# Spreading a row over 128 partitions with one-hot matmuls and ScalarE copies in place of GpSimd's partition broadcast

## The chip, the cores and the metric

The kernel runs on one core of a Trainium2 chip. The metric is the device time of one execution in microseconds (us), from the device's own clock. The kernel before takes 2005.57 us (median of 3 runs, 2004.93 to 2007.7).

Engine names in the profile: PE is TensorE (matmul), PEld its weight loads, DVE VectorE, ACT ScalarE, POOL GpSimd, SP SyncE, which here only issues DMAs. L1267 is line 1267 of the kernel.

## The reference

Two blocks run one after the other on 256 tokens of width 1024, all in float32. The first block is two hybrid layers (a gated convolution, latent attention and dilated attention, merged by gates). The second is one transformer block with conditioning, and it is the one that matters here:

```
mod = silu(c) @ w_ada + b_ada                    # one row of 6*1024
sh1, sc1, gt1, sh2, sc2, gt2 = split(mod, 6)     # six rows of 1024
h = rms_norm(x, g_attn) * (1 + sc1) + sh1
x = x + gt1 * (concat(gqa(h), diff_att(h)) @ w_o)
h2 = rms_norm(x, g_ffn) * (1 + sc2) + sh2
x = x + gt2 * moe(h2)                            # 32 experts, top 4 of each token
return rms_norm(x, g_final)
```

The rows gt1, sh2, (1 + sc2)*g_ffn, gt2 and g_final are each one row of 1024 that multiplies or is added to every token. Tokens lie on the 128 partitions (two tiles of 128 tokens), so each of these rows has to stand in all 128 partitions.

## The kernel before

One instruction stream per engine; each engine takes its instructions in order and waits on semaphores. The order within an engine is made by a scheduler at build time, from priorities and an estimate of times, so an edit can move instructions far from it.

**Where the rows come from.** A side task (`ada`) forms the six rows beside the first block. Four of them end in a tile `modr` of 128 x 2 x 512, zero but for the partitions 0, 32, 64 and 96: partition 32*j holds one half row for each of two slots. `mod_row(i, dst)` (L850) spreads a row to all partitions in two halves of 512 with GpSimd's `partition_broadcast` (L854). Five rows are spread, in nine broadcasts:

- gt1 into the buffer `M`, at the start of the second block (`mod_row(0, ...)`, L1049, just behind the first projection);
- sh2 into `sh` and (1+sc2)*g_ffn into `a`, near the end of the grouped-query attention, when two work tiles come free (`mod_row(1, ...)`, `mod_row(2, ...)`);
- gt2 into `kaT` and `va` at the start of the expert part (L1267). GpSimd then multiplies the experts' output bias `bi` by it (L1269);
- g_final into a weight buffer that has just come free (L1306), beside the last pair of experts.

**What GpSimd does besides.** It computes the reciprocal square root of each token's norm as a power of -0.5: `rm` at L129 (for the block's first norm and for the router, one instruction for each token tile) and `rs_p` at L137.

**The second block.** First norm of both tiles (`rm`, then `XM` scaled by it on VectorE at L227), transposes of `XM` on TensorE (L243), projections, the two attentions, the output projection, the router for tile 0 and tile 1 (`router`, L1158 on), and the expert part. In the router VectorE needs `rm` for the modulated row (`vb`, L1203) and for the logits (`lg`, L1189); the choice of experts and the dispatch matmuls (L1356), which gather each expert's tokens into `xT`, follow from these. Where a row is printed, `mk` is the mask of chosen experts, `sl` their slots, `tri` a triangle matrix for a running count.

**The expert part.** Sixteen pairs of experts; each needs 24 weight tiles of 1 MB, which SyncE loads in a fixed order (L1250, `mload`) into 19 buffers (`mv`, `mhch`, `mhcl`, `mXM`, `mr`, `mw` and so on) in turn. Most of these are work tiles of the second block, and a load waits until its buffer has been read for the last time. TensorE takes the tiles in the same order: 16 input tiles for both experts (L1368), SwiGLU on VectorE and ScalarE, 8 output tiles (L1448; in the last pair L1438), and the combination by gates (L1293).

PSUM has four banks under the tag `mm` for all projections, scores and dispatch matmuls; the expert part holds two of them for the pair in work (L1332 puts the input bias in with a one-hot matmul).

Of the kernel before, what the change touches and what calls it, by code (L numbers as in the profile page):

```python
# [8 lines left out]
F32 = mybir.dt.float32  # L9
# [3 lines left out]
AF = mybir.ActivationFunctionType  # L13
# [10 lines left out]
NEW, TB, YB = 3, 2, 1  # L24
# [5 lines left out]
class Net:  # L30
# [739 lines left out]
    def ada(self):  # L770
# [76 lines left out]
        nc.vector.scalar_tensor_tensor(sc2, sc2, 1.0, grow, op0=ALU.add, op1=ALU.mult)  # L847
        yield

    def mod_row(self, i, dst):  # L850
        nc = self.nc
        for j in range(2):
            r, jj = i // 2, (i % 2) * 2 + j
            nc.gpsimd.partition_broadcast(dst[:, j * 512:(j + 1) * 512], self.modr[32 * jj:32 * jj + 1, r, :],  # L854
                                          channels=128)

    def kv_proj(self, hh, hl, src):
        nc, tmp, wq = self.nc, self.tmp, self.d["w_qkv"]
# [399 lines left out]
    def moe(self, ctx):  # L1258
        tc, nc, d = self.tc, self.nc, self.d
        T = self.tmp = ctx.enter_context(tc.tile_pool(name="moet", bufs=2))  # L1260
        P = ctx.enter_context(tc.tile_pool(name="moe", bufs=1))
        new = [P.tile([128, 2048], F32, name=f"mw{i}") for i in range(NEW)]
        rg = [self.ring.tile([128, 2048], F32, name="mr", tag="raw") for _ in range(3)]
        self.mbufs += rg + new + ["Y1"]
        gt2 = [self.kaT, self.va.rearrange("p b n -> p (b n)")]
        for h in range(2):
            nc.gpsimd.partition_broadcast(gt2[h], self.modr[32 * h + 64:32 * h + 65, 1, :], channels=128)  # L1267
            bh = self.bi[0:32, h * 512:(h + 1) * 512]
            nc.gpsimd.tensor_tensor(bh, bh, gt2[h][0:32], op=ALU.mult)  # L1269
        sl, gt = self.sl, self.gt  # L1270
        self.h2 = self.bigs["vb"].rearrange("p (t n) -> p t n", t=2)
        gT = P.tile([32, 2, 128], F32, name="gT")
        yp = ctx.enter_context(tc.tile_pool(name="yps", bufs=1, space=PSUM))
        acc = [[yp.tile([128, 512], F32, name=f"y{t}{h}") for h in range(2)] for t in range(2)]

        def base():
            p = self.mm_ps([32, 2, 128])
            for t in range(2):
                nc.tensor.transpose(p[:, t], gt[:, t], self.ident)
            nc.scalar.activation(gT, p, AF.Copy)  # L1280
            for t in range(2):
                for h in range(2):
                    hs = slice(h * 512, (h + 1) * 512)
                    nc.tensor.matmul(acc[t][h], self.ident, self.x[:, t, hs], start=False, stop=False)
                    nc.tensor.matmul(acc[t][h], gT[:, t], self.bi[0:32, hs], start=False, stop=False)

        hp = self.hp0
        steps = self.dispatch_steps(sl[:, :, 0:2], gt[:, :, 0:2])
        disp = next(steps)
        for q in range(16):  # L1290
            nxt = None if q in (QO, 15) else (sl[:, :, 2 * q + 2:2 * q + 4], gt[:, :, 2 * q + 2:2 * q + 4])
            disp, hp = self.pair(disp, nxt, [self.onehot(min(2 * q + i, 31)) for i in range(3)], hp, self.mtile, gt2,
                                 lambda t, h, a, b: nc.tensor.matmul(acc[t][h], a, b, start=(q == 0), stop=(q == 15)),  # L1293
                                 steps if q == 0 else (), q == 15)
            if q == 0:
                self.counts()
                base()
            if q == QO:
                while self.mn < 24 * q + 24 + len(self.mbufs) - 1:
                    self.mload()  # L1300
                self.overflow(P, gt2, acc)
                hp = self.in_bias(self.onehot(2 * q + 2))
                disp = self.dispatch(*(v[:, :, 2 * q + 2:2 * q + 4] for v in (sl, gt)))
        buf = self.mbufs[self.mn % len(self.mbufs)]
        gfin, junk = buf[:, 0:1024], buf[:, 1024:1536]
        nc.gpsimd.partition_broadcast(gfin, self.bi[96:97], channels=128)  # L1306
        h2 = self.h2
        ss = [T.tile([128, 2], F32, name="ss", tag="rss", bufs=2) for _ in range(2)]
        square = lambda t, h: nc.scalar.activation(junk, acc[t][h], AF.Square, scale=0.03125, accum_out=ss[t][:, h:h + 1])
        hs = [slice(0, 512), slice(512, 1024)]  # L1310
        for t in range(2):
            square(t, 0)
            nc.vector.tensor_tensor(h2[:, t, hs[0]], gfin[:, hs[0]], acc[t][0], op=ALU.mult)
        for t in range(2):
            square(t, 1)
            r = self.rmean(T, ss[t])
            nc.vector.tensor_tensor(h2[:, t, hs[1]], gfin[:, hs[1]], acc[t][1], op=ALU.mult)
            nc.scalar.activation(h2[:, t, hs[0]], h2[:, t, hs[0]], AF.Copy, scale=r)
            nc.vector.tensor_scalar(h2[:, t, hs[1]], h2[:, t, hs[1]], r, None, op0=ALU.mult)  # L1319
            for h in range(2):  # L1320
                nc.sync.dma_start(self.out[0, t * 128:(t + 1) * 128, hs[h]], h2[:, t, hs[h]])
# [74 lines left out]
    def pair(self, disp, nxt, oh, hp, tile_of, gt2, acc, steps=(), last=False):  # L1396
        nc, T = self.nc, self.tmp
        xT, gs = disp
        hs = [slice(0, 64), slice(64, 128)]
        for k in range(8):  # L1400
            if k == 4:
                for _ in steps:
                    pass
            self.in_tile(hp, xT, tile_of(), k, hs[0])
        ln0 = self.swiglu(hp)
        hp = self.in_bias(oh[1])
        aT = []
        for k in range(8):
            mm = self.in_tile(hp, xT, tile_of(), k, hs[1])
            if k == 2:  # L1410
                with self.tc.issue_after(mm.ins):
                    aT.append(self.act_T(ln0, last))
                    gsT = T.tile([128, 2, 128], F32, name="gsT", tag="gsT", bufs=1)
                    p = self.mm_ps([128, 2, 128])
                    for t in range(2):
                        nc.tensor.transpose(p[:, t], gs[:, t].rearrange("p e c -> p (e c)"), self.ident)  # L1416
                    nc.scalar.activation(gsT, p, AF.Copy)
        ln1 = self.swiglu(hp)
        hp = None
        if nxt is not None:  # L1420
            with self.tc.issue_after(mm.ins):
                nxt = self.dispatch(*nxt)
        aT.append(self.act_T(ln1, last))
        yp = [self.mm_ps([128, 512]) for _ in range(2)]
        ys = T.tile([128, 2, 512], F32, name="ys", tag="ys", bufs=YB)

        def combine(h):
            nc.vector.tensor_tensor(ys[:, h], gt2[h], yp[h], op=ALU.mult)  # L1428
            for t in range(2):
                acc(t, h, gsT[:, t], ys[:, h])  # L1430

        for f in range(4):
            w = [tile_of() for _ in range(2)]
            if last:
                h, q = divmod(f, 2)
                for c in range(4):
                    for e in range(2):
                        nc.tensor.matmul(yp[h][hs[e]], aT[e][:, c, hs[q]], w[e][:, c * 512:(c + 1) * 512],  # L1438
                                         start=(q == 0 and c == 0), stop=(q == 1 and c == 3))
                if q == 1:  # L1440
                    combine(h)
                continue
            for cc in range(2):
                c, q = (f * 2 + cc) % 4, f // 2
                for h in range(2):
                    for e in range(2):
                        o = cc * 1024 + h * 512
                        nc.tensor.matmul(yp[h][hs[e]], aT[e][:, c, hs[q]], w[e][:, o:o + 512],  # L1448
                                         start=(f == 0 and cc == 0), stop=(f == 3 and cc == 1))
        if nxt is not None:  # L1450
            hp = self.in_bias(oh[2])
        if not last:
            for h in range(2):
                combine(h)
        return nxt, hp
# [161 lines left out]
```

## Time and profile before

| | us |
|---|---|
| median of 3 runs | 2005.57 |
| profiled execution, its time | 2004.15 |
| profiled execution, span of the trace | 2002.5 |
| TensorE busy | 1907.1 (95%) |
| VectorE busy | 916.5 (46%) |
| ScalarE busy | 609.9 (30%) |
| GpSimd busy | 411.6 (21%) |
| DMA, expert part from slice 25 of 40 on | 420 to 421 GB/s |

The profile's page gives busy times of the whole span. TensorE's share is modelled: matmuls overlap, so it shows when TensorE had something in work and not how fast it was. The timeline gives one engine's or all engines' instructions in order of start; what stands in brackets is how long the engine had been idle before, and what ended it, `issue` where no semaphore in the profile did. The windows give the busy time of each engine in a stretch, the mean granted clock of TensorE as a share of 2.4 GHz, and what the DMA engines moved.

### The profile page before, as it was taken

Reading aid. Unit: us, or ns where it says so; the run is one execution under the profiler, and the core shown is the slowest. Engines: PE = TensorE matmul, PEld = TensorE weight load, DVE = VectorE, ACT = ScalarE, POOL = GpSimd, SP = SyncE. Lnnn points to the kernel's source line nnn. Section 1 sums busy time; section 2 is a strip of 40 time slices with the busy share of each in tenths; the row PEclk is TensorE's granted clock in tenths of the full one; section 3 lists DMA queues with packets and bytes.
Section 4 is the critical chain, followed back from the end, with each engine's and each line's share of the span. In section 5 each row is a group of like instructions: output and inputs, shape, how many; then the busy total and the mean of one; then the engine's idle time right before and its main releaser. Section 6 shows DMA issues by size and latency. Waiting matters only on the chain. (4 is left out here: it accounts for less than half of the span.)

```text
span 2002.5 us, 25915 instructions
## 1 busy us (share of the span) xinstructions
PE 1907.1 (95%) x10323; PEld 1182.0 (59%) x10323; DVE 916.5 (46%) x1728; ACT 609.9 (30%) x1099; POOL 411.6 (21%) x334
## 2 busy tenths in 40 slices
PE   6989999989899999889978999999999998999997
PEld 6878988978679889776654333333333333433332
DVE  6798778588976665768762011111111101111102
ACT  4646445546465454545551000000000000100001
POOL 3135336663345235411220000000000000000000
PEclk8999999999999999989998999999999999999999
DMA  6544544645556444544567999999999999999997
GB/s 225 185 140 159 190 158 148 211 168 198 171 169 212 137 160 159 192 148 147 168 231 291 407 380 421 421 420 420 421 421 421 420 421 420 420 421 421 421 421 291
DMA packets 138452, 568.59 MB, mean 284 GB/s; under 512 B 10603, under 2 KB 16747, under 8 KB 90198
## 3 DMA queue, kind: packets, MB, share of 16 engines
q1 hardware_dynamic: 129664, 540.69, 69.9%
q0 software_dynamic: 6912, 25.17, 3.8%
q8 instruction: 83, 1.36, 0.3%
q10 hardware_dynamic: 1750, 1.03, 0.2%
q14 instruction: 43, 0.35, 0.0%
HBM read 565.79 MB, written 1.05 MB: 283 GB/s over the span
## 5 line engine op out<-in xcount | busy, mean ns | idle before, releaser
L158 DVE TENSOR_TENSOR wl<-raw,wh 128x1024 fp32r<-128x1024 f32 (+3 forms) x255 | 339.2, 1334 | 126.8 <-ACT wh L156 123.0
L156 ACT ACTIVATE wh<-raw 128x1024 fp32r<-128x1024 f32 (+3 forms) x255 | 262.8, 1034 | 236.5 <-PE mm L181 217.1
L182 PE MATMUL mm<-hh,wl 128*128 128x256 f32 x768 | 220.6, 289 | 0.0
L181 PE MATMUL mm<-hl,wh 128*128 128x256 f32 x768 | 220.2, 287 | 0.0
L1379 ACT ACTIVATE modr<-g 128x512 f32<-128x512 f32 x32 | 20.2, 630 | 655.7 <-DVE g L1378 655.7
L180 PE MATMUL mm<-hh,wh 128*128 128x256 f32 x768 | 219.8, 287 | 0.0
L1378 DVE TENSOR_SCALAR g<-mm 128x512 f32<-128x512 f32 x32 | 22.1, 692 | 409.3 <-PE mm L1368 409.3
L1306 POOL PARTITION_BROADCAST mtb<-bi x1 | 1.3, 1307 | 893.6 <-PE mm L1368 893.6
L181 PE MATMUL mm<-wl,hh 128*128 128x512 f32 (+2 forms) x424 | 171.5, 405 | 11.3 <-DVE wl L158 11.2
L182 PE MATMUL mm<-wh,hl 128*128 128x512 f32 (+2 forms) x424 | 169.3, 400 | 2.4 <-DVE hl L216 2.1
L180 PE MATMUL mm<-wh,hh 128*128 128x512 f32 (+2 forms) x424 | 162.6, 406 | 6.6 <-ACT hh L248 3.5
L822 POOL TENSOR_TENSOR araw<-araw,tb 128x1024 f32<-128x1024 f32 x48 | 104.7, 2180 | 299.0 <-DVE part L818 123.2
L182 PEld LDWEIGHTS mm<-hh,wl 128*128 128x128 f32 x768 | 144.3, 189 | 6.4 <-issue 4.7
L180 PEld LDWEIGHTS mm<-hh,wh 128*128 128x128 f32 x768 | 144.9, 189 | 4.7 <-issue 4.2
L181 PEld LDWEIGHTS mm<-hl,wh 128*128 128x128 f32 x768 | 144.7, 188 | 3.4 <-issue 2.0
L1428 DVE TENSOR_TENSOR ys<-kaT,mm 128x512 f32<-128x512 f32 x16 | 11.0, 688 | 276.7 <-PE mm L1448 266.3
L181 PEld LDWEIGHTS mm<-wl,hh 128*128 128x128 f32 x424 | 84.7, 200 | 31.4 <-DVE wl L158 14.1
L180 PEld LDWEIGHTS mm<-wh,hh 128*128 128x128 f32 x424 | 84.0, 200 | 26.4 <-ACT hh L248 5.2
L182 PEld LDWEIGHTS mm<-wh,hl 128*128 128x128 f32 x424 | 84.2, 199 | 19.6 <-DVE hl L216 3.1
L824 POOL TENSOR_TENSOR araw<-araw 128x512 f32<-128x512 f32 x48 | 82.6, 1720 | 3.8
L1356 PE MATMUL mm<-modr,vb 128*128 128x128 f32 x512 | 65.8, 289 | 14.7 <-DVE lg L1189 14.1
L1368 PE MATMUL mm<-mr,xT 128*64 128x512 f32 x328 | 78.1, 604 | 1.7 <-DMA mr<-in_w_in_dram 1.7
(444 smaller groups left out, 3577.1 us busy)
## 6 DMA issues: line engine op xcount, KB each, us to landing
raw<-in_w_in_dram SPq DMA_DIRECT2D x84, 1024.0 KB, 5.1
mr<-in_w_in_dram SPq DMA_DIRECT2D x41, 1024.0 KB, 18.2
mw<-in_w_in_dram SPq DMA_DIRECT2D x39, 1024.0 KB, 19.8
mv<-in_w_in_dram SPq DMA_DIRECT2D x27, 1024.0 KB, 19.8
mY<-in_w_in_dram SPq DMA_DIRECT2D x26, 1024.0 KB, 19.8
araw<-in_w_ada_dram POOLq DMA_DIRECT2D x48, 512.0 KB, 4.4
mw<-in_w_out_dram SPq DMA_DIRECT2D x21, 1024.0 KB, 19.2
mr<-in_w_out_dram SPq DMA_DIRECT2D x19, 1024.0 KB, 19.9
```

Of the source, the lines that this page charges most:

```text
L156: nc.scalar.activation(wh, src, AF.Copy)
L158: eng.tensor_tensor(wl, src, wh.bitcast(F32), op=ALU.subtract)
L180: nc.tensor.matmul(out, sh, mh, start=first, stop=False, skip_group_check=skip)
L181: nc.tensor.matmul(out, sh, ml, start=False, stop=False, skip_group_check=skip)
L182: nc.tensor.matmul(out, sl, mh, start=False, stop=last, skip_group_check=skip)
L822: nc.gpsimd.tensor_tensor(raw, raw, cT[:, 0, kh * 4:kh * 4 + 4, None].to_broadcast([128, 4, 256]), op=ALU.mult)
L824: nc.gpsimd.tensor_tensor(raw[:, 0:2], raw[:, 0:2], raw[:, 2:4], op=ALU.add)
L1356: nc.tensor.matmul(p[:, j], self.h2[:, t, k * 128:(k + 1) * 128], sx[:, t].rearrange("p e c -> p (e c)"), start=(t == 0 and j == 0), stop= ...
L1368: mm = self.nc.tensor.matmul(hp[i][h * 64:h * 64 + 64], xT[:, k, cols], w[:, o:o + 512], start=False, stop=(k == 7))
L1378: nc.vector.tensor_scalar(g, hg, 7.0, None, op0=ALU.min)
L1379: nc.scalar.activation(th, g, AF.Tanh, scale=0.851)
L1428: nc.vector.tensor_tensor(ys[:, h], gt2[h], yp[h], op=ALU.mult)
```

## The change

All nine broadcasts are replaced by ten pairs of a matmul and a copy. `spread` takes 32 partitions of `modr`, of which only the first is not zero, and multiplies them by a column of the identity that is repeated 128 times: every partition of the PSUM bank receives the row. ScalarE copies the bank to where the broadcast wrote before. For g_final the contraction has one partition, the result has its own tile (in the buffer that held `xT`), it is made inside the last pair's function, and the scratch tile `junk` of the last norm is a work tile of its own and no longer part of a weight buffer.

```diff
+    def spread(self, row, jj, dst, ps):
+        rows = slice(32 * jj, 32 * jj + 32)
+        self.nc.tensor.matmul(ps, self.ident[rows, 32 * jj:32 * jj + 1].to_broadcast([32, 128]), row[rows],
+                              start=True, stop=True)
+        self.nc.scalar.activation(dst, ps, AF.Copy)
+
     def mod_row(self, i, dst):
         for j in range(2):
             r, jj = i // 2, (i % 2) * 2 + j
-            nc.gpsimd.partition_broadcast(dst[:, j * 512:(j + 1) * 512], self.modr[32 * jj:32 * jj + 1, r, :],
-                                          channels=128)
+            self.spread(self.modr[:, r, :], jj, dst[:, j * 512:(j + 1) * 512], self.mm_ps([128, 512]))
...
         for h in range(2):
-            nc.gpsimd.partition_broadcast(gt2[h], self.modr[32 * h + 64:32 * h + 65, 1, :], channels=128)
+            self.spread(self.modr[:, 1, :], h + 2, gt2[h], self.mm_ps([128, 512]))
             bh = self.bi[0:32, h * 512:(h + 1) * 512]
             nc.gpsimd.tensor_tensor(bh, bh, gt2[h][0:32], op=ALU.mult)
...
-        buf = self.mbufs[self.mn % len(self.mbufs)]
-        gfin, junk = buf[:, 0:1024], buf[:, 1024:1536]
-        nc.gpsimd.partition_broadcast(gfin, self.bi[96:97], channels=128)
+        gfin = self.gfin
+        junk = T.tile([128, 512], F32, name="junk", tag="g", bufs=TB)
...
+        if last:
+            self.gfin = T.tile([128, 1024], F32, name="gfin", tag="xT", bufs=1)
+            for h in range(2):
+                p, js = self.mm_ps([128, 512]), slice(h * 512, h * 512 + 512)
+                nc.tensor.matmul(p, self.ident[96:97, 96:97].to_broadcast([1, 128]), self.bi[96:97, js],
+                                 start=True, stop=True)
+                nc.scalar.activation(self.gfin[:, js], p, AF.Copy)
         aT.append(self.act_T(ln1, last))
```

GpSimd at the start of the second block, where `rm` is the norm's reciprocal root for both token tiles and `M` is where gt1 goes; `ISA` rows without a tile are control instructions of GpSimd:

```order
 L761 MEMSET lg 128x2x4
 L759 CAST tri<-trif 128x128
-L854 ISA
-L854 ISA M<-modr 128x512 x2
-L129 ISA
 L129 TENSOR_TENSOR rm<-ss,mhalf 128x1 x2
 L137 TENSOR_TENSOR rs_p<-hss,mhalf 128x4 x2
```

The two broadcasts and the control instructions on either side of them are gone from in front of `rm`.

GpSimd at the router, before the change, from tile 0's `rm` to the branch of the expert part:

```order
L129 TENSOR_TENSOR rm<-ss,mhalf 128x1
L1267 ISA
L1267 ISA kaT<-modr 128x512
L1267 ISA va<-modr 128x512
L1269 ISA
L1269 TENSOR_TENSOR bi<-bi,kaT 32x512
L129 TENSOR_TENSOR rm<-ss,mhalf 128x1
L1269 TENSOR_TENSOR bi<-bi,va 32x512
L1461 TENSOR_LOAD cni
```

And the same place after it:

```order
L137 TENSOR_TENSOR rs_p<-dfs,mhalf 128x1 x5
L129 TENSOR_TENSOR rm<-ss,mhalf 128x1 x2
L1273 TENSOR_TENSOR bi<-bi,kaT 32x512
L1273 TENSOR_TENSOR bi<-bi,va 32x512
L1471 TENSOR_LOAD cni
```

Tile 1's `rm` stood behind the broadcasts, two control instructions and the first bias product; it now stands right behind tile 0's, and no control instruction is left between them.

TensorE at the same place, before the change: `cst,lT` makes tile 1's logits, `modr,vb` are dispatch matmuls, `mv` and `mhch` the first two weight tiles:

```order
L1184 MATMUL mm<-h2T,rt 32x128 x8
L1188 MATMUL mm<-cst,lT 128x32
L1356 MATMUL mm<-modr,vb 128x128 x8
L1199 LDWEIGHTS tri
L1199 MATMUL at<-mk,tri 128x32
L1356 MATMUL mm<-modr,vb 128x128 x8
L1368 MATMUL mm<-mv_8426,xT 64x512 x4
L1368 MATMUL mm<-mhch,xT 64x512 x4
```

And after it (line numbers of the changed file):

```order
L1188 MATMUL mm<-h2T,rt 32x128 x8
L1192 MATMUL mm<-cst,lT 128x32
L852 MATMUL mm<-modr,ident 128x512 x2
L1203 LDWEIGHTS tri
L1203 MATMUL at<-mk,tri 128x32
L1359 MATMUL mm<-modr,vb 128x128 x16
L1371 MATMUL mm<-mv_8426,xT 64x512 x4
L1371 MATMUL mm<-mhch,xT 64x512 x4
```

The two spread matmuls of gt2 take the place of tile 0's eight dispatch matmuls, which now stand behind the count with `tri`.

## Rows read from the trace of the kernel before

**Rows 1.** Page, part 2: DMA rate in 40 slices of the span.

```profile
GB/s 225 185 140 159 190 158 148 211 168 198 171 169 212 137 160 159 192 148 147 168 231 291 407 380 421 421 420 420 421 421 421 420 421 420 420 421 421 421 421 291
```

**Rows 2.** Windows: stretch, length; busy PE, PEld, DVE, ACT, POOL; clock, DMA share, GB/s.

```profile
850.00:860.00 10.00, 0.66 (x3) 0.66 (x4) 1.39 (x2) 0.00 (x0) 2.12 (x4) 0.56 0.00 0
859.35:865.00 5.65, 5.65 (x25) 5.46 (x26) 5.64 (x8) 0.00 (x0) 0.00 (x0) 0.50 0.30 93
870.00:1030.00 160.00, 156.20 (x817) 110.09 (x816) 122.92 (x286) 94.80 (x204) 31.04 (x33) 1.00 0.52 172
1046.00:1048.00 2.00, 0.00 (x0) 0.00 (x0) 0.00 (x0) 0.00 (x0) 0.00 (x0) 0.50 0.41 156
1050.00:1064.00 14.00, 7.28 (x31) 5.88 (x33) 5.48 (x18) 1.51 (x3) 3.06 (x3) 0.54 0.00 0
1200.00:1975.00 775.00, 761.55 (x3436) 290.38 (x3434) 105.98 (x173) 51.79 (x95) 1.31 (x1) 0.99 1.01 420
```

**Rows 3.** Timeline, all engines, 843 to 860 us: start, length, instruction, idle before.

```profile
846.18 0.21 DVE L128 TENSOR_SCALAR ss<-ss 128x1 f32<-128x1 f32 x1 [0.40 <-ACT XM L225]
...
847.29 0.28 PE L182 MATMUL mm<-wh,hcl 128*128 128x256 f32 x1
849.22 1.48 POOL L854 PARTITION_BROADCAST M<-modr  x2 [5.60 <-issue]
857.91 1.42 POOL L129 TENSOR_TENSOR rm<-ss,mhalf 128x1 f32<-128x1 f32 x2 [7.21 <-issue]
858.54 1.58 DVE L227 TENSOR_SCALAR XM<-x,rm 128x1024 f32<-128x1024 f32 x2 [12.14 <-POOL rm L129]
859.35 0.90 PE L243 MATMUL at<-ident,XM 128*128 128x128 f32 x3 [11.77 <-DVE XM L227]
```

**Rows 4.** Timeline, all engines, 1036 to 1066 us: the router's end.

```profile
1036.77 0.20 DVE L128 TENSOR_SCALAR ss<-ss 128x1 f32<-128x1 f32 x1
...
1040.63 0.41 PE L1188 MATMUL mm<-cst,lT 128*128 128x32 f32 x2 [0.46 <-ACT lT L1186]
...
1040.88 1.14 PE L1356 MATMUL mm<-modr,vb 128*128 128x128 f32 x8
...
1051.62 1.25 POOL L1269 TENSOR_TENSOR bi<-bi,kaT 32x512 f32<-32x512 f32 x1 [11.18 <-issue]
1052.85 0.59 POOL L129 TENSOR_TENSOR rm<-ss,mhalf 128x1 f32<-128x1 f32 x1
...
1055.82 0.24 DVE L1189 SCALAR_TENSOR_TENSOR lg<-mm,rm,cst 128x32 f32<-128x32 f32 x1
...
1056.11 2.08 PE L1356 MATMUL mm<-modr,vb 128*128 128x128 f32 x8 [14.09 <-DVE lg L1189]
...
1062.54 2.11 PE L1368 MATMUL mm<-mv,xT 128*64 128x512 f32 x8
...
1064.69 0.33 SPq L1250 DMA_DIRECT2D mv<-in_w_out_dram  x1
```

**Rows 5.** Prices: two timeline rows of TensorE, one group of ScalarE by form.

```profile
1036.49 1.09 PE L1332 MATMUL mm<-bi,ident 32*64 32x512 f32 x8
...
1932.60 1.98 PE L1293 MATMUL y<-ys,gsT 128*128 128x512 f32 x4
...
L1359 ACT ACTIVATE xT<-mm 128x512 f32<-128x512 f32 x4 | 2.4, 597 | 7.8 <-PE mm L1356 7.8
```

**Rows 6.** Timeline, 974 to 978.5 us: where sh2 and its scale are spread.

```profile
974.28 1.03 PE L902 MATMUL at<-ident,araw 128*128 128x128 f32 x8
...
977.02 1.09 ACT L600 ACTIVATE pT<-at 128x512 f32<-128x512 f32 x2 [0.36 <-PE at L599]
...
977.73 0.43 PE L960 MATMUL o<-pT,va 128*64 128x128 f32 x2
```

**Rows 7.** The end: two tiles of the last pair on TensorE, and g_final's broadcast.

```profile
1960.84 1.94 PE L1368 MATMUL mm<-mv,xT 128*64 128x512 f32 x8 [0.36 <-DMA mv<-in_w_in_dram]
...
1968.34 1.94 PE L1368 MATMUL mm<-mr,xT 128*64 128x512 f32 x8 [0.58 <-DMA mr<-in_w_in_dram]
...
L1306 POOL PARTITION_BROADCAST mtb<-bi x1 | 1.3, 1307 | 893.6 <-PE mm L1368 893.6
```

More of the change, by code (lines that the diff above doesn't have):

```diff
@@ L848, in ada @@
         yield
+    def spread(self, row, jj, dst, ps):
[3 more added lines that the diff above has]
+        self.nc.scalar.activation(dst, ps, AF.Copy)
     def mod_row(self, i, dst):
-        nc = self.nc
         for j in range(2):
             r, jj = i // 2, (i % 2) * 2 + j
-            nc.gpsimd.partition_broadcast(dst[:, j * 512:(j + 1) * 512], self.modr[32 * jj:32 * jj + 1, r, :],
-                                          channels=128)
+            self.spread(self.modr[:, r, :], jj, dst[:, j * 512:(j + 1) * 512], self.mm_ps([128, 512]))
     def kv_proj(self, hh, hl, src):
```

## The prediction

> **What bounds the kernel now.** I read the DMA rate by slices first. From the 25th of 40 slices on it stands at 420 to 421 GB/s [rows 1]; over 1200 to 1975 us the DMA engines are busy throughout, share 1.01 at 420 GB/s [rows 2]. There the stream of expert weights sets the pace, and nothing that GpSimd, ScalarE or TensorE does within it counts. What does count is when this stream starts to run without a break, and the reader is to see that this is late: between 1050 and 1064 us the rate is 0 GB/s, with all buffers full and TensorE busy for 7.28 us of 14 [rows 2]. SyncE issues the next load at 1064.69 us, 0.04 us after the first weight tile has been multiplied (1062.54 + 2.11) [rows 4]. So every microsecond by which the first expert matmul comes earlier moves the whole stream, as long as the DMA engines are idle in that time. They are from about 1047 us on (156 GB/s in 1046 to 1048) to 1064.7, some 17.7 us.
>
> Ahead of the expert part TensorE is the bound: 156.2 of 160 us busy from 870 to 1030 [rows 2]. Two holes in it stand out in the timeline, and both end with GpSimd.
>
> First hole: TensorE waits 11.77 us for `XM`, VectorE waits 12.14 us for `rm`, and GpSimd runs `rm` at 857.91 after 7.21 us in which no semaphore held it; before that it spent 5.60 us in the same way and 1.48 us on two broadcasts [rows 3]. Its input `ss` had been ready since 846.18 + 0.21 = 846.39.
>
> Second hole: TensorE waits 14.09 us for the logits `lg`, which need tile 1's `rm`. Its input was ready at 1036.77 + 0.20 = 1036.97; `rm` ran at 1052.85, behind a bias product that GpSimd began only after 11.18 us without a semaphore to wait for [rows 4]. In the order of instructions these unexplained stretches lie between a broadcast and the next ordinary GpSimd instruction, where the control instructions stand. I read them as GpSimd changing the code that it runs.
>
> The Trainium skill ("GPSIMD Engine Reference", section 2.1 Instruction dispatch) states that the first call into freshly loaded GpSimd code costs about 6 us more, without an instruction in the profile. The way into the broadcast agrees (5.60 us); the ways back took 7.21 and 11.18 us here, longer than that page's figure. With 6 us for the second way back, the second gain below would be 5.2 us smaller and the time 1986.2 us; the measured rows decide.
>
> **The change, part by part.** Nine broadcasts and their control instructions leave GpSimd; ten matmuls of 512 columns and ten ScalarE copies come in.
>
> *Price of one pair.* The trace before has no such matmul. The nearest rows: four bias matmuls of 512 columns with 32 rows each, on two row groups and two column groups, take 1.09 us together; two matmuls of 128 rows and 512 columns, one behind the other, take 1.98 us [rows 5]. Halves of one row lie in different row groups, so I take 1.1 us for such a pair or for the four at 975 us, and keep serial execution (0.95 us each after the first) as the dear end. A ScalarE copy of 512 columns out of PSUM takes 0.60 us [rows 5].
>
> *gt1, at the first hole.* The two spread matmuls stand directly ahead of the transposes on TensorE. They need `modr`, which the broadcast had as well. TensorE ends its earlier work at 847.29 + 0.28 = 847.57, so the transposes start at about 848.7. By then `XM` is there: `ss` at 846.39, one `rm` of about 0.6 us [rows 4], half of 1.58 us for the first tile [rows 3], sum 847.8. The gain is 859.35 - 848.7 = 10.65 us. Bounds: 9.8 with serial matmuls (1.9 us), 11.8 if they cost nothing. Beside it, TensorE ran at half clock, 0.50 (1.2 GHz), from 859.35 to 865.00, after the pause [rows 2]. At 2.4 GHz these 5.65 us would be 2.8 shorter at most, but VectorE was busy for 5.64 us of them, so I count 1.0, bounds 0 and 2.8.
>
> *sh2 and its scale, at 975 us.* No hole goes here: `sh` was there in time. The four matmuls stand between two groups of transposes of `araw` (1.03 us together), and four copies, 4 x 0.60 = 2.4 us, stand ahead of the copy of `pT` at 977.02, on which the matmuls at 977.73 hang [rows 6]. TensorE is the bound, so this costs: 1.1 us by TensorE alone, 2.4 us by ScalarE's queue, up to 5 if the four matmuls run serially (3.8) and a copy follows. I take 2.5, nearest to the copies; bounds 0 and 5.
>
> The Trainium skill ("TensorEngine Tiling (Array Packing)", PSUM Bottleneck) warns that packed small matmuls can leave the copy out of PSUM as the bottleneck. The rows point the same way here, 2.4 us of copies against 1.1 us of matmuls; by TensorE's row alone the time would be 1.4 us shorter.
>
> *gt2, at the second hole.* Now `rm` follows at 1037.0 and ends at 1037.6, and `lg` waits for TensorE's product instead, which ends at 1040.63 + 0.41 = 1041.04 [rows 4]. So `lg` starts at 1041.1 and not at 1055.82. Behind it, on TensorE: one spread matmul waits for the bank that `lg` reads (0.24 us) and takes 1.1, the count with `tri` 0.2, then all 32 records of the dispatch, at 1.14 us for eight records at full clock [rows 4] 4.5 us. The first expert matmul starts at 1041.1 + 0.24 + 1.1 + 0.2 + 4.5, about 1047.2, against 1062.54: 15.3 us. Bounds: 13.6 if the old 6.72 us from `lg` to the first expert matmul stay and the spread comes on top; 16.5 if the spread is hidden. The copies of gt2 (1.2 us) fall while TensorE counts and dispatches. The gain fits into the 17.7 us of idle DMA time.
>
> *g_final.* Its broadcast waited 893.6 us for its buffer and lay beside the stream [rows 7]. Its two matmuls, serial in one row group, 1.9 us, now stand in TensorE's queue ahead of the tile `mv` of the last pair. TensorE waits for a DMA ahead of each of the four tiles there, 0.36 us at the first and 0.58 us at the last [rows 7], about 2 us in all, so they are absorbed; without that cover they cost 1.9 us. I count 0.
>
> *The order elsewhere.* The scheduler also permutes attention instructions from 860 to 1030 us, with the same work. TensorE idles there for 3.8 us in 160 [rows 2]; that is the most it can win, and I allow as much loss. I count 0.
>
> **Sum.** 10.65 + 1.0 - 2.5 + 15.3 = 24.45 us. From the profiled execution's 2004.15 us that gives 1979.7. The median of the runs lies 1.4 us above that execution, so I forecast 1981. Ends: least gain 9.8 + 0 - 5 + 13.6 - 3.8 = 14.6, time 1991; most gain 11.8 + 2.8 - 0 + 16.5 + 3.8 = 34.9, time 1971. What is late next: in the first hole VectorE's splits and transposed tiles; in the second the product that ends at 1041.04; behind both the stream.
>
> **The rivals.**
>
> *Only the second hole pays.* Behind the first hole VectorE is full (5.64 of 5.65 us), and the weights for the next projections come through a ring of three buffers that filled up during the hole (0 GB/s in 850 to 860 [rows 2]). If these fill the time that is freed, perhaps 3 us of the first gain are left: 2005.57 - 3 + 2.5 - 15.3 = 1989.8. Against it: VectorE's burst at 858.5 is work that had piled up behind the late `rm`.
>
> *Only the first hole pays*, because the weight tiles are not there: 2005.57 - 11.65 + 2.5 = 1996.4. Against it: 0 GB/s from 1050 to 1064.
>
> *The unexplained waits belong to `modr` and not to GpSimd's code.* Then the spread matmuls on TensorE wait for the same thing, in an in-order queue with the transposes behind them, and the change does not do what it says. Both holes stay, and their price is added: 1.1 + 2.5 + 1.1, so 2010, slower than before. It decides if the transposes still start at or after 859 us. Against it: two different ways back from a broadcast, after which no `modr` is read, show the longest of these waits.
>
> **How the numbers follow.** Forecast as summed 0.78, first rival 0.11, second 0.04, third 0.04, something else 0.03. Less than 0.2% (4 us) either way is about what measurement here can't tell from no change. Faster by over that: the first three and most of the rest, 0.94; within it 0.02; slower 0.04. The range 1971 to 1992 holds the forecast with its bounds and the first rival.
>
> **What would show it.** Right: no GpSimd gap of 5 us or more between 840 and 1060; `rm` within 2 us of its `ss`; transposes of `XM` about 1 us behind the end of the first projection; TensorE never idle for over 3 us between 860 and the expert part, its clock at 1.00 there; the first expert matmul some 24 us earlier, and the load behind it too; the DMA rate without a stretch at 0 before it; the stretch from the first expert matmul to the end as long as now (2002.5 - 1062.5 = 940 us). Wrong: a new wait of TensorE at the spread matmuls, for a bank or for ScalarE, of over 2 us; `kaT` or `sh` copies on which something waits; or an expert part that is longer by what was won before it, which would mean that the stream was the bound from earlier on than I read.

## The result, and the profile after

The changed kernel takes 1980.03 us (median of 4 runs, 1977.79 to 1981.92) against 2006.63 before: ratio 0.9857, 95% interval 0.9823 to 0.9891. Timed again on two other occasions the ratio was 0.9857 [0.9831, 0.9883] and 0.9887 [0.9873, 0.9901]. So it is faster, by what was forecast (1981 us). How that came about needs more care, because some terms missed in opposite directions.

Part 2 of the page of the changed kernel, the DMA rate in 40 slices, answers to [rows 1]: the steady 420 GB/s begin in the same slice, of a shorter span (1979.8 us against 2002.5).

```profile
GB/s 208 191 139 180 172 158 171 186 157 209 172 164 201 168 131 155 201 201 149 170 234 367 421 381 421 420 421 421 421 421 421 421 421 420 420 421 420 422 421 288
```

The windows of the changed kernel (columns as in [rows 2]) show both holes filled: TensorE is busy for all of 850 to 860 us (0.66 us before), at a granted clock of 1.00. The last row is the end of the routing, and there the clock is not 1.00.

```profile
850.00:860.00 10.00, 10.00 (x64) 8.22 (x63) 9.77 (x14) 7.41 (x11) 1.12 (x2) 1.00 0.35 107
852.34:858.00 5.66, 5.66 (x41) 5.17 (x40) 5.66 (x9) 3.07 (x6) 0.00 (x0) 1.00 0.60 180
870.00:1030.00 160.00, 154.05 (x846) 107.37 (x844) 122.56 (x295) 95.59 (x205) 26.70 (x31) 1.00 0.54 183
1036.00:1042.00 6.00, 6.00 (x29) 4.46 (x30) 0.58 (x2) 1.19 (x2) 0.00 (x0) 0.67 0.04 15
```

The timeline of the changed kernel at the first hole, answering to [rows 3]: `rm` follows its `ss` at once, and the `XM` transposes start 1.27 us behind the start of the last matmul of the first projection (12.06 before). The two spread matmuls (L852) show as x4, since each of them leaves two records.

```profile
849.48 0.21 DVE L128 TENSOR_SCALAR ss<-ss 128x1 f32<-128x1 f32 x1 [0.19 <-ACT XM L225]
...
849.77 1.40 POOL L129 TENSOR_TENSOR rm<-ss,mhalf 128x1 f32<-128x1 f32 x2 [0.93 <-DVE ss L128]
...
851.07 0.28 PE L182 MATMUL mm<-wh,hcl 128*128 128x256 f32 x1
...
851.28 1.13 PE L852 MATMUL mm<-modr,ident 32*128 32x512 f32 x4
...
852.34 0.87 PE L243 MATMUL at<-ident,XM 128*128 128x128 f32 x6
```

And at the second hole, answering to [rows 4]: `lg` stands 0.45 us behind the product that it needs (15.19 before), but from `lg` to the first expert matmul it now takes 9.39 us (6.72 before).

```profile
1026.49 0.55 POOL L129 TENSOR_TENSOR rm<-ss,mhalf 128x1 f32<-128x1 f32 x1 [5.73 <-DVE ss L128]
...
1030.07 0.41 PE L1192 MATMUL mm<-cst,lT 128*128 128x32 f32 x2 [0.46 <-ACT lT L1190]
...
1030.41 1.53 PE L852 MATMUL mm<-modr,ident 32*128 32x512 f32 x4
1030.52 0.25 DVE L1193 SCALAR_TENSOR_TENSOR lg<-mm,rm,cst 128x32 f32<-128x32 f32 x1 [0.97 <-PE mm L1192]
...
1032.24 1.26 POOL L1273 TENSOR_TENSOR bi<-bi,kaT 32x512 f32<-32x512 f32 x1 [5.21 <-ACT kaT L854]
1032.27 1.27 DVE L1216 TENSOR_SCALAR gt<-gt,smr 128x32 f32<-128x32 f32 x1
...
1033.47 1.25 POOL L1273 TENSOR_TENSOR bi<-bi,va 32x512 f32<-32x512 f32 x1
1033.67 1.20 DVE L1351 TENSOR_TENSOR modr<-cst,sl 128x128 f32<-128x128 f32 x1
...
1034.92 5.06 PE L1359 MATMUL mm<-modr,vb 128*128 128x128 f32 x22 [0.98 <-DVE modr L1351]
...
1039.91 1.94 PE L1371 MATMUL mm<-mv,xT 128*64 128x512 f32 x8
```

Cut at the same instructions, the two traces compare like this (starts to starts, us):

| stretch | before | after | won |
|---|---|---|---|
| start of the span to last matmul of the first projection | 847.29 | 851.07 | -3.78 |
| to the first `XM` transposes (first hole) | 12.06 | 1.27 | 10.79 |
| to the `araw` transposes | 114.93 | 109.74 | 5.19 |
| to the product of `cst` and `lT`, tile 1 | 66.35 | 67.99 | -1.64 |
| to `lg` | 15.19 | 0.45 | 14.74 |
| to the first expert matmul | 6.72 | 9.39 | -2.67 |
| to the end of the span | 939.96 | 939.89 | 0.07 |

The first row is not the change: up to there TensorE's instructions stand in one order in every kernel but one below (the one that computes `rm` otherwise), and yet in twelve profiled executions the first of the two `ss` in front of the hole came between 845.3 and 857.1 us. That scatter goes straight into the time, so the experiments are read by their stretches, and by medians only where the difference is large. Without that row the trace shows 26.5 us won; the medians show 26.6.

### The profile page after: what moved, and what is told of

Its sections match the earlier page's. It is cut to its first block, busy times and chain, and to the rows that moved or that the text cites. A ratio compares the mean times of both kernels' runs of the same rounds, so it can differ in the third digit from the quotient of the medians.

```text
span 1979.8 us, 25923 instructions
## 1 busy us (share of the span) xinstructions
PE 1909.1 (96%) x10343; PEld 1185.1 (60%) x10343; DVE 918.6 (46%) x1728; ACT 615.8 (31%) x1109; POOL 403.4 (20%) x325
## 5 line engine op out<-in xcount | busy, mean ns | idle before, releaser
L129 POOL TENSOR_TENSOR rm<-ss,mhalf 128x1 f32<-128x1 f32 x10 | 6.3, 630 | 962.3 <-DVE ss L128 958.9
L180 PEld LDWEIGHTS mm<-wh,hh 128*128 128x128 f32 x424 | 84.4, 200 | 26.6 <-ACT hh L248 4.1
L1359 PEld LDWEIGHTS mm<-modr,vb 128*128 128x128 f32 x512 | 63.6, 206 | 14.5 <-issue 13.0
```

Of the source, the lines that this page charges most:

```text
L180: nc.tensor.matmul(out, sh, mh, start=first, stop=False, skip_group_check=skip)
L1359: nc.tensor.matmul(p[:, j], self.h2[:, t, k * 128:(k + 1) * 128], sx[:, t].rearrange("p e c -> p (e c)"), start=(t == 0 and j == 0), stop= ...
```

## The experiments

**One hole at a time.** In three kernels made from the one before, one group of rows alone goes to TensorE. The first makes gt1 by `spread`, the third, with `if i:` in the same place, sh2 and the scale; the second has only the last two lines:

```diff
+            if i == 0:
+                self.spread(self.modr[:, r, :], jj, dst[:, j * 512:(j + 1) * 512], self.mm_ps([128, 512]))
+            else:
...
-            nc.gpsimd.partition_broadcast(gt2[h], self.modr[32 * h + 64:32 * h + 65, 1, :], channels=128)
+            self.spread(self.modr[:, 1, :], h + 2, gt2[h], self.mm_ps([128, 512]))
```

*gt1 alone:* 

> The kernel before with only gt1's broadcast made by spread; sh2, scale, gt2 and g_final stay on GpSimd. Theory (GpSimd's change of code makes each hole by itself): last matmul of the first projection to the XM transposes 1.3 us instead of 12.06, TensorE's granted clock 1.00 in the ten us behind them, XM transposes to araw transposes 110 us instead of 114.9 (3.0 of that is the clock of 0.73 that stands there before), and the second hole stays: cst,lT to lg 15 us, lg to the first expert matmul 6.7. Time 15 us under the kernel before, some 1990. Rival (the waits belong to modr): rm still comes 8 to 11 us behind ss, time within 3 us of before. Rival (the 5.2 us between the XM and the araw transposes came from the new places of the sh2 and scale rows, not from the first hole): that stretch stays 115 and the gain is 10.8.

Measured: 1990.61 us against 2007.67, ratio 0.9913 [0.9894, 0.9933]. The first hole is 1.27 us, the next stretch 109.74, both as in the full change, though sh2 and the scale are still on GpSimd here. The second hole stands as before: 14.92 us, `lg` to the first expert matmul 6.34. Both rivals fall.

*gt2 alone:* 

> The kernel before with only gt2's broadcast made by spread. Theory: the first hole stays (12 us between the last matmul of the first projection and the XM transposes, the stretch behind them 115), cst,lT to lg falls from 15.19 to 0.5, lg to the first expert matmul is 9.4 as in the changed kernel (TensorE takes the spread pair ahead of the eight dispatch matmuls, and GpSimd's product with bi runs beside VectorE's small ones). Time 12 us under the kernel before, some 1994. Rival (waits belong to modr): rm stays behind, time within 3 us of before. Rival (9.4 comes from what happens earlier in the changed kernel, not from this edit): lg to the first expert matmul 6 to 7, time 15 us under before.

Measured: 1991.42, ratio 0.9916 [0.9899, 0.9933]. First hole 12.27 and next stretch 114.89, as before; `lg` 0.45 us behind its product. From `lg` to the first expert matmul it was 6.89 and not 9.4, with TensorE's order as in the full change: so 9.39 is not fixed by the order. (VectorE's `gt` took 1.29 us beside GpSimd's product here, but `modr`, which started 0.01 us ahead of the second product, took 0.28.) The median fell by more than expected (16.3 against 12); the trace gives 14.6 us between the product and the first expert matmul.

*sh2 and the scale alone:* 

> The kernel before with only the rows sh2 and scale by spread. Theory: both holes stay as they were (12 and 15 us), the four spreads cost 1.1 to 2.5 us of TensorE and the span is 0 to 3 us longer, some 2005 to 2008. Rival (the order that the scheduler finds without the GpSimd calls gives the 5.2 us): XM to araw transposes 110 instead of 115 and the time 3 to 5 us under before. Rival (the GpSimd calls cost here too): GpSimd's wait ahead of its add to x falls and the time is 2 us or more under before.

Measured: 2009.0, ratio 1.0005 [0.999, 1.002]: no difference. Both holes remain (12.75 and 14.93), the stretch to `araw` is 115.47, and from there to the product 68.69 against 66.35. These four broadcasts cost nothing on GpSimd, and moving them costs about 2 us of TensorE's way.

**The waits without `modr`.** The rows are spread by TensorE, and GpSimd gets three calls that read a constant:

```diff
+        nc.gpsimd.partition_broadcast(self.gt1[:, 0:128], self.ident[0:1, :], channels=128)
         self.mod_row(0, self.gt1)
...
+            nc.gpsimd.partition_broadcast(gt2[h][:, 0:128], self.ident[0:1, :], channels=128)
             self.spread(self.modr[:, 1, :], h + 2, gt2[h], self.mm_ps([128, 512]))
```

> The changed kernel with three GpSimd broadcasts of a constant row (128x128, from the identity, nothing of modr) put where gt1's and gt2's stood in GpSimd's order; the rows are still made by spread, which overwrites what the calls wrote. Theory (the change of code between a broadcast and the next ordinary instruction): both holes come back although no GpSimd instruction reads modr: rm 7 us or more behind the first calls, 8 to 12 us between the last matmul of the first projection and the XM transposes, 12 to 15 us between cst,lT and lg, time 20 to 26 us over the changed kernel, 2000 to 2007. Rival (the waits belong to modr, or to 128x512 rows being copied): the holes stay away or return by under 3 us each, time 1980 to 1986.

Measured: 2001.62 us, ratio to before 0.9979 [0.9964, 0.9995]; more than three quarters of the gain is gone. The holes are back: 11.82 us ahead of the `XM` transposes, and 11.08 from the product to `lg`, a little less than the 12 to 15 expected. The timeline of this kernel, at both places:

```profile
850.18 0.43 POOL L1053 PARTITION_BROADCAST M<-ident  x1 [5.92 <-issue]
...
857.60 1.41 POOL L129 TENSOR_TENSOR rm<-ss,mhalf 128x1 f32<-128x1 f32 x2 [6.99 <-issue]
...
859.03 1.97 PE L243 MATMUL at<-ident,XM 128*128 128x128 f32 x8 [10.48 <-DVE XM L227]
...
1037.72 0.43 POOL L1272 PARTITION_BROADCAST va<-ident  x1
...
1048.53 0.59 POOL L129 TENSOR_TENSOR rm<-ss,mhalf 128x1 f32<-128x1 f32 x1 [10.38 <-issue]
...
1050.48 0.25 DVE L1194 SCALAR_TENSOR_TENSOR lg<-mm,rm,cst 128x32 f32<-128x32 f32 x1
```

A call on 128 columns of a constant brings 5.92 us in and 6.99 and 10.38 us back, as 512 columns of `modr` did (5.60; 7.21, 11.18). The waits belong to the switch and not to the data. Why one way back takes 7 us and the other 10 to 11 no run shows. The profile has a mark for it that I had not read before: grouped by source line, GpSimd's own queue lists a control instruction. In the kernel before, the line of the bias product shows it right behind the broadcasts, and the product 11 us later (columns: durations in ns, first and last start):

```profile
L1269 POOLq MODIFY_POOL_CONFIG  x2: 127/127/127, 1040.3 to 1040.4; - x2
...
L1269 POOL TENSOR_TENSOR bi<-bi,kaT x1: 1255/1255/1255, 1051.6 to 1051.6; 32x512 f32<-32x512 f32 x1
```

In the changed kernel the line of `rm` keeps only the pair at the program's start (six before):

```profile
L129 POOLq MODIFY_POOL_CONFIG  x2: 37/37/37, 3.0 to 3.1; - x2
```

The Trainium skill ("GPSIMD Engine Reference", section 2.1 Instruction dispatch) counts its roughly 6 us from this same control instruction to the first call of the freshly loaded code, less the wait for events. The way in agrees (5.6 to 5.9 us here); the ways back, 7.0 to 11.2 us in these runs, are longer than its figure.

**Leave the switch, take `rm` off its way.** The kernel before, with `rm` on VectorE:

```diff
...
-        nc.gpsimd.tensor_tensor(y, ss[:, 0:1], self.mhalf[:, 0:1], op=ALU.pow)
+        nc.vector.tensor_scalar(i, a.bitcast(I32), 1, None, op0=ALU.arith_shift_right)
+        nc.vector.tensor_scalar(y.bitcast(I32), i, -1.0, float(0x5F3759DF), op0=ALU.mult, op1=ALU.add)
+        for _ in range(3):
+            nc.vector.scalar_tensor_tensor(t, y, -0.5, y, op0=ALU.mult, op1=ALU.mult)
+            nc.vector.tensor_tensor(t, t, a, op=ALU.mult)
+            nc.vector.scalar_tensor_tensor(y, t, 1.5, y, op0=ALU.add, op1=ALU.mult)
```

> The kernel before, all broadcasts on GpSimd, but rm worked out on VectorE by eleven small instructions (shift, and three Newton steps) in all its places instead of one GpSimd power. Theory (the hole is the wait of whichever ordinary GpSimd instruction follows a broadcast, and it costs only because rm is on the path): the wait of 7 us moves to GpSimd's rs_p and that of 11 to its bi product; last matmul of the first projection to the XM transposes 2 to 4 us instead of 12.06, cst,lT to lg 0.5 to 3 instead of 15.19; 20 to 24 us gained there, 2 to 6 given back at the other norms, time 1984 to 1992. Rival (other instructions behind rm wait for GpSimd just as long, rs_p of the key norm or M's row): the first hole shrinks by under 4 us or returns as a TensorE pause of over 5 us later, time 1995 or more.

Measured: 1979.46 us, ratio 0.9862 [0.9833, 0.9892], the same gain as the change, with every broadcast left on GpSimd; better than I expected. From the product to `lg` it takes 1.15 us, inside what was expected; from `lg` to the first expert matmul only 4.44, against 6.72 before, which I had not counted; and its score matmuls stand in the new order (below), with 2.3 us less of TensorE's time. What the eleven small instructions cost at the other norms was not measured by itself. Its timeline shows the wait still there, at an instruction for which nobody waits:

```profile
853.48 2.95 POOL L860 PARTITION_BROADCAST M<-modr  x2 [5.90 <-issue]
...
1032.63 0.24 DVE L1195 SCALAR_TENSOR_TENSOR lg<-mm,rm,cst 128x32 f32<-128x32 f32 x1
...
1037.07 1.94 PE L1374 MATMUL mm<-mv,xT 128*64 128x512 f32 x8
...
1041.11 1.26 POOL L1275 TENSOR_TENSOR bi<-bi,kaT 32x512 f32<-32x512 f32 x1 [11.00 <-issue]
```

The bias product comes 4 us behind the first expert matmul. TensorE was busy for 10.00 us of 850 to 860 here: where `XM` is late, it has other work, in another order.

**The 9.39 us.** First the changed kernel again, unedited, twice.

> The changed kernel once more, for a second profile and more times on the chip of its variants. Theory (the 9.39 us from lg to the first expert matmul is partly the collision of GpSimd's bi product with VectorE's small instructions and the low TensorE clock that follows, both of which vary): 7 to 9.4 us here, time 1978 to 1982. Rival (9.39 is set by the order alone): within 0.4 us of 9.39.

> The changed kernel a third time, beside the next two on the same chip: 1978 to 1982; lg to the first expert matmul between 7.06 and 9.39 us as in its two profiles so far.

Measured: 1980.88 and 1982.51 us; `lg` to the first expert matmul 7.06 us both times, so the rival falls. The timeline of the first of these two, against the one above:

```profile
1033.01 1.27 DVE L1216 TENSOR_SCALAR gt<-gt,smr 128x32 f32<-128x32 f32 x1
...
1034.41 1.20 DVE L1351 TENSOR_TENSOR modr<-cst,sl 128x128 f32<-128x128 f32 x1
...
1035.66 2.72 PE L1359 MATMUL mm<-modr,vb 128*128 128x128 f32 x22 [1.33 <-DVE modr L1351]
...
1038.32 1.94 PE L1371 MATMUL mm<-mv,xT 128*64 128x512 f32 x8
```

The stretched VectorE instructions come back each time; the 22 matmuls take 2.72 us or 5.06. That difference, 2.34, is TensorE's clock: granted 1.00 throughout in this execution, half (1.2 GHz) in the first, for most of 1033 to 1040. The engine's work ahead of it was the same.

Nor was the first execution alone in this. Two variants below (the products alone; g_final back on GpSimd) have TensorE's instructions in the same order up to the first expert matmul, and the clock fell in both. The windows from `lg` to the first expert matmul, in the order first profile of the changed kernel, second, products alone, g_final:

```profile
1030.52:1039.91 9.39, 8.26 (x37) 6.77 (x37) 4.70 (x15) 2.00 (x4) 2.48 (x2) 0.64 0.61 254
...
1031.26:1038.32 7.06, 5.58 (x38) 4.29 (x38) 4.70 (x15) 2.00 (x4) 2.48 (x2) 1.00 0.81 339
...
1031.77:1040.39 8.62, 8.50 (x37) 6.80 (x37) 4.70 (x15) 2.11 (x4) 2.48 (x2) 0.60 0.68 283
...
1030.73:1038.12 7.39, 7.03 (x38) 5.63 (x38) 4.71 (x15) 2.00 (x4) 2.48 (x2) 0.77 0.79 332
```

So the steady cost is 7.06, and in three of five profiles a lower clock added 0.3 to 2.3 us to it. What decides whether it falls stays open.

To find the steady part, the two GpSimd products were moved into `base()`, behind the first pair of experts (the line taken out below stands there unchanged); then, in a second kernel, the spread pair as well, into `pair()`:

```diff
-            nc.gpsimd.tensor_tensor(bh, bh, gt2[h][0:32], op=ALU.mult)
...
+            if k == 5 and self.late:
+                with self.tc.issue_after(mm.ins):
+                    for h in range(2):
+                        self.spread(self.modr[:, 1, :], h + 2, self.late[h], self.mm_ps([128, 512]))
```

*Products alone:* 

> The changed kernel with GpSimd's two products of bi with gt2 issued behind the first pair of experts instead of beside the last routing steps; TensorE's order is unchanged. Theory (the products stretch VectorE's gt and modr instructions from 0.24 and 0.29 us to 1.27 and 1.20): these take 0.24 and 0.29 again, lg to the first expert matmul 6.5 to 7.5 us, time 1 to 3 us under the changed kernel, 1977 to 1980. Rival (the low clock of TensorE alone makes the 9.39, the stretched instructions are cover): lg to the first expert matmul 8.5 or more, time the same within 1.

Measured: 1980.9, ratio 0.9865 [0.984, 0.989], the same. The edit did not do what it says: GpSimd had nothing queued ahead, so it ran the products as soon as gt2 was there (1033.49, beside `gt` at 1033.52, again 1.27 us long). From `lg` to the first expert matmul it took 8.62 us, at a mean clock of 0.60. No verdict on either theory.

*Spread pair and products:* 

> As the run before it, and gt2's spread pair with its ScalarE copies issued behind the sixth input tile of the first pair of experts, where TensorE waits for loads anyway; ahead of the last routing step TensorE's order is then that of the kernel before (eight dispatch matmuls before the matmul with tri, eight behind). Theory: lg to the first expert matmul 5.9 to 6.5 us, the spread pair costs nothing in the stream, the first expert matmul is 3 us earlier than in the changed kernel against the end of the first projection, and the time 2 to 4 us less, 1976 to 1978. Rival (the stream is bound by its loads from their first issue, not from the first expert matmul): from the first expert matmul to the end takes 3 us more than 940, time the same within 1.

Measured: 1982.21, ratio 0.9867 [0.9843, 0.989], no faster. Its timeline:

```profile
1038.83 0.24 DVE L1216 TENSOR_SCALAR gt<-gt,smr 128x32 f32<-128x32 f32 x1
...
1039.20 0.29 DVE L1351 TENSOR_TENSOR modr<-cst,sl 128x128 f32<-128x128 f32 x1
...
1039.55 2.05 PE L1359 MATMUL mm<-modr,vb 128*128 128x128 f32 x16 [0.62 <-DVE modr L1351]
...
1041.53 1.94 PE L1371 MATMUL mm<-mv,xT 128*64 128x512 f32 x8
```

With neither beside them the VectorE instructions take 0.24 and 0.29 us, and `lg` to the first expert matmul 4.45: the theory holds there. But from the first expert matmul to the end it now takes 943.1 us instead of 940: in the windows, the rate 40 to 60 us behind that matmul is 327 GB/s, where the changed kernel has 389 (1079.91 to 1099.91) and the other profiles 376 to 398:

```profile
1081.53:1101.53 20.00, 20.00 (x92) 6.46 (x92) 1.38 (x2) 0.00 (x0) 0.00 (x0) 1.00 0.81 327
```

The first pair is no idle place: TensorE is busy for all 20 us. That the spread pair put there holds up the loads behind it is argued from this rate and not shown by itself. So the rival is right in this half, as far as one profile can say: from the first expert matmul to the end took 937.9 to 941.4 us in the other profiles.

*gt2 early,* as soon as the grouped attention has read `kaT` and `va` for the last time (the lines leave their old place, and the first router tile's transposes go to other buffers):

```diff
         self.drain(ga)
+        for h in range(2):
+            self.spread(self.modr[:, 1, :], h + 2, gt2[h], self.mm_ps([128, 512]))
+            bh = self.bi[0:32, h * 512:(h + 1) * 512]
+            nc.gpsimd.tensor_tensor(bh, bh, gt2[h][0:32], op=ALU.mult)
...
```

> The changed kernel with gt2's spread pair and GpSimd's two products of bi issued as soon as the grouped attention is done with kaT and va, some 60 us ahead of the routing (the first router tile keeps its transposes in other buffers for that). Theory (what is left at the second hole is the spread pair in front of the dispatch matmuls, GpSimd's products beside VectorE's gt and modr, and the low TensorE clock behind both): lg to the first expert matmul 4.45 us as where the pair stood in the first pair of experts, the pair costs 0 to 1.2 us where it now is, the stream from the first expert matmul to the end 940 as before, so 2 to 4 us less than the changed kernel, 1976 to 1978. Rival (the stretch from the first expert matmul to the end grows by what was won, as the 943 of that run says): 943 and the same time within 1.

Measured: 1979.02 us, ratio 0.9883 [0.9859, 0.9908], beside 0.9887 for the unedited kernel on the same chip: the same within the scatter. The stretches say what the medians can't: `lg` to the first expert matmul 4.45 us, the stream 939.7, but `araw` to the product 69.53 against 67.99. Of 2.61 us won on 7.06, 1.5 is paid some 60 us earlier.

*g_final back on GpSimd* (its broadcast into a weight buffer, and no spread in the last pair):

> The changed kernel with the row of the last norm put back on GpSimd, into a weight buffer. Theory (the old call and its wait lay under the last expert matmuls, while its reader came later): time the same within 1 us; TensorE loses the two spread matmuls of the last pair, 1.1 us that nothing waited for. Rival (the call's change of code delays rm of the last norm): rm stands 5 us or more behind the last ss and the time is 3 to 6 us longer.

Measured: 1982.32 us, ratio 0.99 [0.9869, 0.9931], the same. The broadcast runs at 1922.18 and the last norm's `rm` at 1969.41, 0.15 us behind its `ss`.

## Why the prediction held, and where it did not

**The cause** was right. Constant data brings the holes back, and moving `rm` alone removes their cost, so they are GpSimd's switch between broadcasts and ordinary instructions, on the way to `rm`. The rival of `modr` is out, and so are the two that let only one hole pay: alone, each gave 16 to 17 us. Together that is 33, more than the 26.6 of the full change. Of the 6.7 between, the traces name 2.5 (9.39 us behind `lg` against 6.89) and about 2 (sh2 and the scale); the rest is no larger than the scatter.

**gt1:** 10.65 forecast, 10.79 measured, and 1.13 us for the pair against 1.1.

**The clock behind the first hole** was mis-sized: 1.0 forecast, 2.6 measured. The kernel with constant calls has TensorE's order of the changed kernel with the hole in it; there the stretch from `XM` to `araw` takes 112.36 us, against 109.74 without the hole. TensorE ran at 0.50 for 5.67 us of it, as the window of that kernel shows:

```profile
859.03:864.70 5.67, 5.67 (x26) 5.58 (x27) 5.66 (x8) 0.47 (x1) 0.00 (x0) 0.50 0.45 111
```

I had discounted this because VectorE was full as well; but VectorE is also full at 1.00 (5.66 us of 5.66 from 852.34 to 858), so its load was no reason to halve the term.

**The order elsewhere** was mis-sized: 0 forecast, 2.6 measured (114.93 to 112.36), inside the bound of 3.8. Most of it can be named. The score matmuls use half of the array's rows; two of them side by side on different halves, a couple, take 1.13 us, as long as one alone (1.12). From the grouped table by form, TensorE, of the kernel before, and of the one with constant calls, whose order is the new one:

```profile
L948 PE MATMUL mm<-kaT,G 64*128 64x512 f32 x32 | 15.5, 635 | 1.4 <-ACT G L931 1.4
```

```profile
L952 PE MATMUL mm<-kaT,G 64*128 64x512 f32 x32 | 13.2, 635 | 1.4 <-ACT G L935 1.4
```

The mean of one is the same, 635 ns; only the busy time falls by 2.3 us, because in two more couples the matmuls stand next to each other. The timeline of the changed kernel has such a couple (four records) and a lone matmul (two):

```profile
934.46 1.13 PE L952 MATMUL mm<-kaT,G 64*128 64x512 f32 x4
...
948.15 1.12 PE L952 MATMUL mm<-kaT,G 64*128 64x512 f32 x2
```

The group takes 13.2 in the changed kernel and in every other experiment, 15.5 in the kernel before, with gt2 alone, and with sh2 and the scale alone. It was a by-product of where the scheduler put things, and it could have gone the other way.

**sh2 and its scale:** cost 2.5 forecast, 1.64 measured (2.3 in the kernel with this part alone).

**gt2:** the step that failed is the way from `lg` to the first expert matmul, forecast as 0.24 + 1.1 + 0.2 + 4.5, about 6.1 us. The first half was exact (`lg` 0.45 us behind its product, 0.47 forecast). The second took 9.39, 7.06 and 7.06, so the gain was 12.1 to 14.4 us instead of 15.3, and the first value lies below my bound of 13.6. The sum has no wait between the spread pair and the dispatch; even at full clock TensorE stood 1.33 us there for `modr`. I had put the spread pair and its copies into the sum and forgotten the two GpSimd products that the copies release. Before, the first stood in front of `rm`, with VectorE idle, and the second ran beside the first half of `vb`, which took 1.76 us there (0.75 in the changed kernel); now they run beside VectorE's `gt` and `modr`, which take 1.27 and 1.20 us instead of 0.24 and 0.29, with TensorE waiting. The Trainium skill ("SBUF — State Buffer", section Who interferes with whom) says that VectorE and GpSimd share a pair of ports, and that of two instructions that both need this pair the one issued later is blocked for the whole of the earlier one. The rows agree: `gt` starts 0.03 us behind a product and both end within 0.04 us, and with gt2 alone, where `modr` came 0.01 us ahead, it is the product that is longer (1.39 us against 1.25). What goes beyond 7.06 is the clock.

**g_final:** 0 forecast, and no difference measured.

**Two signs did not come.** TensorE's clock was not 1.00 up to the expert part in the first profile (0.67 over 1036 to 1042 us), and the DMA rate still falls ahead of it: 15 GB/s over the same stretch, 0 from 1038 on, until SyncE issues the next load at 1041.89, 0.04 us after the first weight tile has been multiplied. So some 4 us of idle DMA time are left there, of the 17.7 before.

**The sum.** Forecast 24.45; measured 10.79 + 2.62 + 2.57 - 1.64 + 12.07 = 26.4 in the first profile; in the two others of the changed kernel, without the low clock, the first expert matmul came 28.8 us earlier, counted from the end of the first projection. The clock, the order and sh2 came out 5.1 us better together, the second hole 3.2 worse. The time was met because these misses nearly cancel, and the reasoning deserves credit for the two holes, not for the last microseconds. The stream was as forecast: 939.89 us from the first expert matmul, 940 predicted.

## What to carry to other kernels

Look at GpSimd's instruction order for custom calls (broadcasts) followed by ordinary instructions on a critical path: here the switch was 5.6 to 5.9 us in, where no semaphore held the call, and 7 to 11 us back, for 128 columns as for 512, and taking either side off GpSimd recovered it. When a wait disappears, list what its end now releases earlier, on the neighbouring engines too, before you sum the rest. And a move into a place where "TensorE waits anyway" needs that place's busy time looked up first.

## What the runs showed that I had not expected

- TensorE's clock after the same instructions fell in three profiled executions (mean 0.60 to 0.77 from `lg` to the first expert matmul) and stayed at 1.00 in two: up to 2.3 us on 22 matmuls.
- The start of the hole scattered by 12 us between executions of the same TensorE instructions (845.3 to 857.1), so differences of a few us between variants show in the stretches and not in the medians.
- Four spread matmuls of 512 columns, each on its own 32 rows, take 1.14 us together, as long as two (1.13).
